# Key transposes placed behind the score products, and the first merge blocks issued as a stream of the front, in a hybrid RWKV7/FoX trunk layer

## The chip, the cores and the metric

The kernel runs on one core of one Trainium2 chip. The metric is the device time of one execution in microseconds. The kernel before was run three times: 827.68, 828.11 and 828.64 us, median 828.11 us. One further execution was profiled; its time was 826.71 us and its trace spans 824.9 us.

TensorE is called PE below, VectorE DVE, ScalarE ACT, GpSimd POOL. A PSUM "bank" is one of the accumulation buffers that PE writes and DVE or ACT reads.

## The reference, cut to what matters

```python
u = rmsnorm(h, norm_mix)
proj = u @ w_in                                  # 1024 -> RWKV features, FoX features, two gates
y_rw = rwkv7_branch(proj[..., :C_RW], ...)       # generalised delta rule, 8 heads of 64
y_fx = fox_branch(proj[..., C_RW:C_RW+C_FX], ...)# forgetting attention, 8 heads of 64
gates = sigmoid(proj[..., C_RW+C_FX:] + b_gate)
merged = gates[..., :1024] * (y_rw @ w_out_rw) + gates[..., 1024:] * (y_fx @ w_out_fx)
h = h + merged @ w_o
h = h + square(relu(rmsnorm(h, norm_mlp) @ w_up)) @ w_down
```

512 tokens and 16 meta tokens, width 1024, everything in float32. One layer.

## The kernel before, in words

Every large product is split: a weight tile `wraw` is cast on ACT to a high part `whi`, DVE subtracts to get the low part `wlo`, and PE runs three passes (`whi` with the high and the low part of the activations, `wlo` with the high part).

The first 400 us are the *front*. Forty projection jobs (function `projections`, matmuls at L582, casts at L550, subtractions at L551) form one stream. Between their matmuls stand the matmuls of the other streams: the recurrent branch with its chain over chunks, the attention, the FoX features, the group norm. Each stream is a Python generator that yields the time at which its next piece can start, by a planner's own costs; the planner takes the most urgent ready stream, and projections have the last rank but one, so that they fill gaps. This fixes PE's order by hand. The orders of DVE, ACT and the queues come from a scheduler. Nothing can overtake on PE: if the instruction at its head waits, PE stands still.

The PSUM banks have names: `pj` (two), `ch` and `py` (one each), and a ring of four called `sm` that serves everything small in the front (`psm`) and the accumulators `po` of the merge and the MLP (`ppo`). A new `sm` tile takes the bank of the fourth one before it and has to wait until that one's readers are done.

The recurrent branch works on four pairs of heads, p = 0 to 3. For a pair, `keys` makes `BK` (L922) and `KT` (L924) on DVE. `scores` goes over nine chunks in three groups of three. A group takes two `sm` banks, `sb` and `sk`, and fills them with 12 products of `BK` and `L` (L964, 24 instructions in the trace, called `psr`); DVE reads `sb` once (`Bm`, L965) and `sk` twice (`L`, L967). Then the group transposes its three chunks of `KT` on PE into a third bank (`pbt`, L971), which ACT copies out (L972, L974).

When a pair's tanh values are done (L261), `pinned` puts a load of another activation table (L268) on ACT, for the logarithms and exponentials that follow.

Behind the front stands the merge: for eight blocks m, two products of four blocks of `ys` each (the RWKV branch, br 0, and the FoX branch, br 1; 24 matmuls at L1267), a gate that comes back from DRAM (`gl`) and goes through tanh (L1262), its product on DVE (L1269), a sum on POOL (L1271) and a split (L1272, L1273). Its weights come through `load_w` (L242), which holds four half-block tiles, so two blocks; block 0 is asked for ahead of the loop, every other block in its own pass.

Of the kernel before, what the change touches and what calls it, by code (L numbers as in the profile page):

```python
# [24 lines left out]
NCH = 9  # L25
HT = T // 2
KB = 8
# [162 lines left out]
def kernel(ctx, tc, ht, x, win, par, cst, gain, lora, wout, wo, wup, wdn, out, dbg=None):  # L190
# [84 lines left out]
    def split(hi, lo, x):  # L275
        return A.copy(hi, x), V.tensor_tensor(lo, x, hi.bitcast(F32), ALU.subtract)  # L276
# [6 lines left out]
    ps = ctx.enter_context(tc.tile_pool(name="ps", bufs=2, space=PSUM))  # L283
    gates_d = [dr.tile([128, S], F32, name=f"gd{i}") for i in range(16)]
    ys = {}
    quarters = [[wdn[i][256 * c:256 * c + 256] for c in range(8)] for i in range(4)]

    with ExitStack() as st:
# [254 lines left out]
        def convert(job, raws):  # L543
# [9 lines left out]
                w.append((hi, lo))  # L553
            return job, w

        def projections(total):
            fetched, done = None, 0
            while done < total:
                if fetched is None:
                    yield lambda: 0.0 if jobs else math.inf  # L560
                    fetched = fetch(jobs.pop(0))
                cur = convert(*fetched)
                fetched = fetch(jobs.pop(0)) if jobs else None
                while cur is not None:
                    (_, _, _, begin, parts, ev, need), w = cur
                    nxt = convert(*fetched) if fetched else None
                    fetched = fetch(jobs.pop(0)) if jobs else None
                    if need is not None:
                        yield need
                    evac = begin()  # L570
                    for a0, a1 in parts:
                        po = None
                        n = 0
                        for k in range(KB):
                            if k % 2 == 0 or a1 - a0 > 300:
                                yield lambda f=po is None: max(ck.ready(*w[k // 4]), block_bank()[0] if f else 0.0)
                            if po is None:
                                tag = block_bank()[2]
                                po = ppj(tag)[:, :a1 - a0]
                                lent.extend([tag] * (tag != "pj"))  # L580
                            for a, b in passes(wk(w, k), U):
                                mm(po, a, b[:, k, a0:a1], start=n == 0, stop=n == 23)  # L582
                                n += 1
                        evac(po, slice(a0, a1))
                        if tag in lent:
                            lent.remove(tag)
                    ev.done = True
                    done += 1
                    cur = nxt

        def gate_job(i):
            def begin():
# [13 lines left out]
        def two(j, k):  # L606
            ys[4 * j + k] = t = kp.tile([128, 2, S], F32R, name="ys", tag=SLOTS[(4 * j + k) // 2], bufs=2)
            return t[:, 0, :], t[:, 1, :]

        def divided():  # L610
            yield chained[1]
            for k in range(2):
                split(*two(0, k), y_rw[:, k, :])
            for k in range(3):
                yield fox_done[k]
                split(*two(1, k), y_fx[:, k, :])
            yield normalised[1][1]
            for k in range(2, 4):
                split(*two(0, k), y_rw[:, k, :])

        forgot = Event()

# [102 lines left out]
        def attention():  # L725
# [3 lines left out]
            for p in range(4):  # L729
# [67 lines left out]
                def mixed():  # L797

                    yield lambda: max(ck.ready(vt, vm, pTm, *pT), banks(1))
                    py = psm("py")  # L800
                    for e, hs in enumerate(hss):
                        mm(py[hs], vm[32 * e:32 * e + 16, hs], pTm[32 * e:32 * e + 16, :], start=True, stop=False)
                    for j, at in enumerate((0, 4, 8, 7)):
                        for e, hs in enumerate(hss):
                            mm(py[hs, 128 * j:], vt[:, j, hs], pT[e][:, at:at + 4 - j, :].rearrange("p a b -> p (a b)"), start=False, stop=j == 3)  # L805
                        if j == 0:
                            yield lambda: 0.0
                    if p < 3:
                        A.copy(y_fx[:, p, :], py)
                    else:  # L810
                        yield chained[1]
                        split(*two(1, 3), py)

                pes = yield from scored(0)
                for i in range(4):
# [39 lines left out]
        class Pair:  # L855
# [96 lines left out]
            def scores(self):  # L952


                BK, L, KT = self.BK, self.L, self.KT
                self.bkT = bkT = kp.tile([128, NCH, 128], F32, name="bkT", bufs=2)
                self.Bm = Bm = kp.tile([128, NCH, 128], F32, name="Bm", bufs=2)
                for c0 in range(0, NCH, 3):
                    yield lambda: max(ck.ready(BK, *L) if c0 == 0 else 0.0, banks(2))
                    sb, sk = [psm("psr").rearrange("p (a b) -> p a b", b=128) for e in range(2)]  # L960
                    for j in range(3):
                        for sp, row, turn in ((sb, 0, 1), (sk, 1, -1)):
                            for (e, hs), os in zip(enumerate(hss), hss[::turn]):
                                mm(sp[os, j, :], BK[hs, c0 + j, row, :], L[e][hs, c0 + j, :], start=True, stop=True)  # L964
                    V.tensor_tensor(Bm[:, c0:c0 + 3, :], sb[:, :3, :], bc(tmask, 1, 3), ALU.mult)  # L965
                    for e, os in enumerate(hss[::-1]):
                        V.tensor_tensor(L[e][os, c0:c0 + 3, :], sk[os, :3, :], bc(tmask[os], 1, 3), ALU.mult)  # L967
                    yield lambda: max(ck.ready(KT) + 1.0, banks(1))
                    pb = psm("pbt").rearrange("p (a b) -> p a b", b=128)
                    for c in range(c0, c0 + 3):  # L970
                        nc.tensor.transpose(pb[:, c - c0, :], KT[:, c, :, :].rearrange("p a b -> p (a b)"), ident)  # L971
                    A.copy(bkT[:, c0:c0 + 3, :64], pb[:, :3, :64])  # L972
                    for hs, os in zip(hss, hss[::-1]):
                        A.copy(bkT[hs, c0:c0 + 3, 64:], pb[os, :3, 64:])  # L974

        def inverse(g, Bms, late):
# [54 lines left out]
            for n, pr_, c in cells:  # L1031
                for e, hs in enumerate(hss):
                    mm(p1[hs, n, :], Tt[qs[2 * e], c, pr_, :], W2[qs[2 * e], n, :], start=True, stop=True)
            for n, pr_, c in cells:
                for q in range(4):
                    mm(p2[qs[q], n, :], W2[qs[q], n, :], Tt[qs[q], c, pr_, half(q)], start=True, stop=True)
# [190 lines left out]
        turns.add(3, fox_features())  # L1227
        turns.add(4, divided())
        turns.add(8, projections(24 + 16))
        for i in range(16):  # L1230
            ask(9, B_GATE + i, gate_job(i), SEQ)
        with tc.manual_schedule(engines={mybir.EngineType.PE}):
# [16 lines left out]

    with ExitStack() as st:  # L1250
        mp = st.enter_context(tc.tile_pool(name="mp", bufs=1))
        ahead = [load_w(wout[0])]
        mhi = mp.tile([128, KB, S], F32R, name="mhi")
        mlo = mp.tile([128, KB, S], F32R, name="mlo")
        table["pin"] = None
        for m in range(KB):
            w = ahead.pop() if ahead else load_w(wout[m])
            pp = []
            for br in range(2):
                g = mp.tile([128, S], F32, name=f"gl{br}", bufs=2)  # L1260
                nc.sync.dma_start(g, gates_d[8 * br + m])
                act(g, g, AF.Tanh, scale=0.5)  # L1262
                po = ppo()
                n = 0
                for k in range(4 * br, 4 * br + 4):
                    for a, b in passes(wk(w, k), (0, 1)):
                        mm(po, a, ys[k][:, b, :], start=n == 0, stop=n == 11)  # L1267
                        n += 1
                V.scalar_tensor_tensor(g, g, 1.0, po, ALU.add, ALU.mult)  # L1269
                pp.append(g)  # L1270
            G.tensor_tensor(pp[0], pp[0], pp[1], ALU.add)  # L1271
            merged = act(mhi[:, m, :], pp[0], AF.Copy, scale=0.5)  # L1272
            V.scalar_tensor_tensor(mlo[:, m, :], pp[0], 0.5, mhi[:, m, :].bitcast(F32), ALU.mult, ALU.subtract)  # L1273
# [17 lines left out]

        pd = [ppo(), ppo(), ppd(), ppd()]
        for b2 in range(4):
            w = load_w(wo[0, b2])
            for i, b1 in [(i, b1) for b1 in range(2) for i in range(4)] if b2 < 3 else [(i, b1) for i in range(4) for b1 in range(2)]:
                k = 2 * b2 + b1
                for n, (a, b) in enumerate(passes(M, w[b1])):
                    mm(pd[i], a[:, k, 128 * i:128 * i + 128], b, start=k == 0 and n == 0, stop=k == 7 and n == 2)  # L1298
# [317 lines left out]
```

## Time and profile before

| | |
|---|---|
| runs | 827.68, 828.11, 828.64 us |
| profiled execution | 826.71 us; span of its trace 824.9 us |
| PE busy | 808.1 us, 98% |
| DVE busy | 607.8 us, 74% |
| ACT busy | 452.5 us, 55% |
| POOL busy | 120.0 us, 15% |
| granted PE clock | 0.99 to 1.00 in every stretch |

How to read it: PE is nearly full, so what counts is how long PE stands still and why. A row of the view of waits names the waiting engine and line, what released it, and the total, the number and the longest of such waits. A row of the timeline gives start, duration, engine, line, operation and, in brackets, the idle time ahead of it with what ended it. A row of the windows gives, for a stretch of time, its length and each engine's busy time in it.

### The profile page before, as it was taken

The page shows a single profiled execution, that of the slowest core. Times are in us where ns is not written, and L with a number is a line of the kernel's source. Part 1 is how long each engine was busy: PE and PEld are TensorE (multiplying, and loading weights), DVE is VectorE, ACT ScalarE, POOL GpSimd, SP SyncE. Part 2 cuts the span into 40 slices and gives each one's busy share as a digit, 9 for nine tenths or more (in the row PEclk, how much of TensorE's full clock was granted, in tenths as well). Part 3 has the DMA queues.
Part 4 walks back from the last instruction along what each step waited for, and adds up shares of the span by engine and source line. Part 5 has one row for each costly group of instructions (what it writes and reads, how often), then busy time and mean ns, then how long its engine had stood idle before and what let it go on. Part 6 is the DMA issues. An engine that isn't in the chain of part 4 may idle for free.

```text
span 824.9 us, 15506 instructions
## 1 busy us (share of the span) xinstructions
PE 808.1 (98%) x5886; PEld 667.3 (81%) x5886; DVE 607.8 (74%) x1196; ACT 452.5 (55%) x941; POOL 120.0 (15%) x124
## 2 busy tenths in 40 slices
PE   8999999998999999999999999999999999999998
PEld 6979887876987886778788889888888888888886
DVE  6797985687779855975267655875698678867988
ACT  7767548766575457664366534664445434543452
POOL 1021000010011000000022003100740174017400
PEclk9999999999999999999999999999999999999999
DMA  7222221211211311223687404533742365236532
GB/s 240 75 71 79 69 92 56 79 40 65 79 52 54 128 46 61 90 66 116 218 289 226 159 0 151 176 82 100 225 150 87 115 221 150 77 118 208 156 107 76
DMA packets 51483, 95.88 MB, mean 116 GB/s; under 512 B 5832, under 2 KB 7240, under 8 KB 51408
## 3 DMA queue, kind: packets, MB, share of 16 engines
q1 hardware_dynamic: 47680, 86.37, 33.0%
q0 software_dynamic: 1280, 4.20, 1.7%
q10 hardware_dynamic: 2448, 4.33, 1.5%
q8 instruction: 46, 0.75, 0.4%
q14 instruction: 29, 0.24, 0.1%
HBM read 88.56 MB, written 6.31 MB: 115 GB/s over the span
## 4 chain that ended last, share of the span: by engine, by line
PE 86%; DVE 5%; ACT 5%; issue 2%; DMA 1%; POOL 0%; DVEq 0%; ACTq 0%; SPq 0%
PE pj L582 22%; PE po L1357 21%; PE po L1484 12%; PE pd L1484 5%; PE po L1267 4%; PE po L1329 3%; PE pj L394 1%; PE pd L1298 1%; PE po L1298 1%; PE psc L751 1%; PE py L805 1%; PE psr L964 1%; PE ppt L788 1%; DVE wlo L551 1%; PE pch L1115 1%
## 5 line engine op out<-in xcount | busy, mean ns | idle before, releaser
L582 PE MATMUL pj<-uhi,whi 128*128 128x264 f32 (+1 forms) x480 | 164.3, 342 | 0.0
L582 PE MATMUL pj<-uhi,wlo 128*128 128x264 f32 (+1 forms) x480 | 153.9, 321 | 1.8 <-DVE wlo L551 1.8
L582 PE MATMUL pj<-ulo,whi 128*128 128x264 f32 (+1 forms) x480 | 153.8, 320 | 0.0
L242 DVE TENSOR_TENSOR wlo<-wraw,whi 128x512 fp32r<-128x512 f32 x84 | 81.0, 973 | 36.8 <-ACT whi L242 36.8
L582 PEld LDWEIGHTS pj<-uhi,whi 128*128 128x128 f32 x480 | 90.7, 189 | 12.9 <-issue 4.4
L582 PEld LDWEIGHTS pj<-uhi,wlo 128*128 128x128 f32 x480 | 90.7, 189 | 8.8 <-DVE wlo L551 2.2
L582 PEld LDWEIGHTS pj<-ulo,whi 128*128 128x128 f32 x480 | 91.0, 190 | 6.7 <-issue 1.6
L1357 PE MATMUL po<-zhi,whi 128*128 128x512 f32 (+1 forms) x248 | 94.8, 382 | 0.0
L1357 PE MATMUL po<-zlo,whi 128*128 128x512 f32 (+1 forms) x248 | 94.8, 382 | 0.0
L1357 PE MATMUL po<-zhi,wlo 128*128 128x512 f32 (+1 forms) x248 | 94.8, 382 | 0.0
L242 ACT CAST whi<-wraw 128x512 fp32r<-128x512 f32 x84 | 51.4, 617 | 53.5 <-PE po L1357 20.3
L551 DVE TENSOR_TENSOR wlo<-wraw,whi 128x512 fp32r<-128x512 f32 x78 | 53.8, 699 | 23.5 <-ACT whi L550 22.6
L550 ACT CAST whi<-wraw 128x512 fp32r<-128x512 f32 x78 | 47.7, 617 | 42.4 <-PE pj L582 41.7
L276 ACT CAST whi<-t 128x512 fp32r<-128x512 f32 x64 | 39.9, 624 | 44.6 <-DVE wlo L276 27.2
L1406 POOL TENSOR_TENSOR t<-traw 128x512 f32<-128x512 f32 x24 | 38.4, 1622 | 173.6 <-DMA traw<-in_wdn 173.6
L1484 PE MATMUL po<-wlo,fhi 128*128 128x512 f32 (+1 forms) x164 | 63.4, 387 | 0.2
L1484 PE MATMUL po<-whi,flo 128*128 128x512 f32 (+1 forms) x164 | 62.8, 384 | 0.0
L1484 PE MATMUL po<-whi,fhi 128*128 128x512 f32 (+1 forms) x164 | 62.3, 384 | 0.0
L276 DVE TENSOR_TENSOR wlo<-t,whi 128x512 fp32r<-128x512 f32 x64 | 43.5, 689 | 24.3 <-ACT whi L276 24.0
L1373 ACT CAST fhi<-R 128x768 fp32r<-128x768 f32 (+1 forms) x32 | 30.2, 945 | 49.1 <-DVE R L1380 26.1
L1357 PEld LDWEIGHTS po<-zlo,whi 128*128 128x128 f32 x248 | 46.6, 188 | 9.1
L1357 PEld LDWEIGHTS po<-zhi,wlo 128*128 128x128 f32 x248 | 46.6, 188 | 9.0
(330 smaller groups left out, 1706.4 us busy)
## 6 DMA issues: line engine op xcount, KB each, us to landing
wraw<-in_win SPq DMA_DIRECT2D x84, 256.0 KB, 2.6
wraw<-in_wup SPq DMA_DIRECT2D x60, 256.0 KB, 3.1
wraw<-in_wdn SPq DMA_DIRECT2D x48, 256.0 KB, 2.7
traw<-in_wdn SPq DMA_DIRECT2D x48, 256.0 KB, 3.5
gd<-gt ACTq DMA_DIRECT2D x16, 256.0 KB, 2.2
wraw<-in_wout SPq DMA_DIRECT2D x16, 256.0 KB, 3.9
gl<-gd SPq DMA_DIRECT2D x16, 256.0 KB, 3.8
traw<-in_wdn POOLq DMA_DIRECT2D x16, 256.0 KB, 3.1
```

The lines of the kernel that those rows point to most:

```text
L242: casts.append((A.copy(hi, raw), low.tensor_tensor(lo, raw, hi.bitcast(F32), ALU.subtract)))
L276: return A.copy(hi, x), V.tensor_tensor(lo, x, hi.bitcast(F32), ALU.subtract)
L550: after(A.copy(hi, raw), last["ACT"])
L551: low[0] = V.tensor_tensor(lo, raw, hi.bitcast(F32), ALU.subtract)
L582: mm(po, a, b[:, k, a0:a1], start=n == 0, stop=n == 23)
L1267: mm(po, a, ys[k][:, b, :], start=n == 0, stop=n == 11)
L1298: mm(pd[i], a[:, k, 128 * i:128 * i + 128], b, start=k == 0 and n == 0, stop=k == 7 and n == 2)
L1329: mm(po, a[:, k, 128 * i:128 * i + 128], b[:, k, :], start=n == 0, stop=n == 23)
L1357: mm(po[:, t0:t1], a, b[:, k, t0:t1], start=n == 0, stop=n == 23)
L1373: A.copy(fhi[:, j, a:b], R[:, a:b])
L1406: eng.tensor_tensor(t, sums[c, pair] if c in (T1, T2) else c, d, ALU.add)
L1484: mm(x[i][:, cols], a[:, k, left, 128 * rows:128 * rows + 128], c[:, cols], start=start and k == 0 and n == 0, stop=stop and k == n_pairs ...
```

## The change

Four edits.

1. `scores`: the transposes leave the loop over the groups. All three groups of products come first, then a loop of its own with the three transposes; the planner's due time for them loses a margin of 1 us.
2. `inverse`: between its two loops of matmuls a `yield` gives the planner a place to put other streams' work.
3. A new stream `merging`, last in rank, which starts when all forty projection jobs have been issued. It issues the matmuls of merge blocks 0 and 1 that need only the first parts of `ys`, block 0 into the two `pj` banks and block 1 into `ch` and `py`. `parted` notes which blocks of `ys` are split. The weights of block 0 are asked for ahead of the last projection job.
4. The merge loop takes over the banks begun there, works on branch 1 ahead of branch 0, and asks for weights two blocks in advance, the first blocks of `wo` among them.

```diff
 def projections(total):
+                    if done == total - 1:
+                        begun.append(load_w(wout[0]))
...
+            projected.done = True
+
+        def merging():
+            yield projected
+            for m in range(2):
+                w = begun.pop() if m == 0 else load_w(wout[m])
+                pos = []
+                for br, ks in ((0, (0, 1)), (1, (4, 5, 6, 7))):
+                    if m:
+                        yield chained[1]
+                    tag = ("pj", ("ch", "py")[br])[m]
+                    yield lambda: max(ck.ready(*w[br]), ck.ring(tag, 1, 1 if m else 2))
+                    po = ppj(tag)
+                    n = 0
+                    for k in ks:
+                        while k not in parted:
+                            yield lambda: math.inf if k not in parted else 0.0
+                        yield lambda: ck.ready(parted[k])
+                        for a, b in passes(wk(w, k), (0, 1)):
+                            mm(po, a, ys[k][:, b, :], start=n == 0, stop=n == 11)
+                            n += 1
+                    pos.append((po, n))
+                under[m] = w, pos
...
 def scores(self):
                         V.tensor_tensor(L[e][os, c0:c0 + 3, :], sk[os, :3, :], bc(tmask[os], 1, 3), ALU.mult)
-                    yield lambda: max(ck.ready(KT) + 1.0, banks(1))
+                for c0 in range(0, NCH, 3):
+                    yield lambda: max(ck.ready(KT), banks(1))
                     pb = psm("pbt").rearrange("p (a b) -> p a b", b=128)
...
 def inverse(g, Bms, late):
+            at = ck.pe
+            yield lambda: at
...
+        turns.add(8, merging())
...
         table["pin"] = None
+        line = [wout[m] for m in range(2, KB)] + [wo[0, b2] for b2 in range(4)]
+        ahead = []
         for m in range(KB):
-            w = ahead.pop() if ahead else load_w(wout[m])
+            w, pos = under.get(m) or (ahead.pop(0), [])
+            ahead.append(load_w(line.pop(0)))
             pp = []
-            for br in range(2):
+            for br in (1, 0):
...
-                po = ppo()
-                n = 0
-                for k in range(4 * br, 4 * br + 4):
+                po, n = pos[br] if pos else (ppo(), 0)
+                for k in range(4 * br + n // 3, 4 * br + 4):
...
         for b2 in range(4):
-            w = load_w(wo[0, b2])
+            w = ahead.pop(0)
+            if line:
+                ahead.append(load_w(line.pop(0)))
```

PE's instructions at the scores of pair p = 0, before (`psr` is a product of a group, `pbt` a transpose of `KT`, `pj` a projection; the bracket names the engines whose results a row waits for):

```order
L971 MATMUL pbt<-cs,KT 128x128 x3
L582 MATMUL pj<-uhi,whi 128x512
L582 MATMUL pj<-ulo,whi 128x512
L582 MATMUL pj<-uhi,wlo 128x512
L582 MATMUL pj<-uhi,whi 128x512
L582 MATMUL pj<-ulo,whi 128x512
L582 MATMUL pj<-uhi,wlo 128x512
L964 MATMUL psr<-L_662,BK 64x128
L964 MATMUL psr<-L_663,BK 64x128
L964 MATMUL psr<-L_662,BK 64x128 [waits DVE_49]
```

and in the changed kernel, from the end of the second group on, where groups one and two stand back to back:

```order
L999 MATMUL psr<-L_662,BK 64x128
L999 MATMUL psr<-L_663,BK 64x128
L587 MATMUL pj<-uhi,whi 128x512
L587 MATMUL pj<-ulo,whi 128x512
L587 MATMUL pj<-uhi,wlo 128x512
L999 MATMUL psr<-L_662,BK 64x128 [waits DVE_49]
L999 MATMUL psr<-L_663,BK 64x128
L999 MATMUL psr<-L_662,BK 64x128 [waits DVE_49,PE_49]
```

with the transposes behind the third group:

```order
L1007 MATMUL pbt<-cs,KT 128x128 [waits DVE_49]
L1007 MATMUL pbt<-cs,KT 128x128 x2
L1007 MATMUL pbt<-cs,KT 128x128 [waits DVE_49,PE_49]
L1007 MATMUL pbt<-cs,KT 128x128 x2
L587 MATMUL pj<-uhi,whi 128x512
L587 MATMUL pj<-ulo,whi 128x512
L587 MATMUL pj<-uhi,wlo 128x512
L1007 MATMUL pbt<-cs,KT 128x128 [waits DVE_49]
```

The transposes moved from between the groups to behind them, and the waits for DVE that a group carried on one row now stand on two rows of the third group and on each transpose.

DVE's instructions at pair p = 1, before (`KT` and `BK` feed the scores, `Bm` and `L` read their banks, `wlo` is a projection's low part):

```order
L921 SCALAR_TENSOR_TENSOR KT<-okk,lc 128x9x64
L306 MEMSET tm 128x1
L922 SCALAR_TENSOR_TENSOR BK<-tha,KT 128x9x64 [waits DVE_49]
L310 SCALAR_TENSOR_TENSOR ov<-pj,pr_65,tm 128x264 [waits DVE_49,Activation_49]
L924 TENSOR_TENSOR KT<-BK,P 128x1152 [waits DVE_49]
L310 SCALAR_TENSOR_TENSOR ov<-pj,pr_65,tm 128x264 [waits Activation_49]
L551 TENSOR_TENSOR wlo<-wraw,whi 128x512 [waits DMAHW5_49,PE_49]
L551 TENSOR_TENSOR wlo<-wraw,whi 128x512 [waits DMAHW6_49,PE_49]
L306 MEMSET tm 128x1 [waits DVE_49]
L965 TENSOR_TENSOR Bm<-psr,cs 128x384 [waits PE_49]
```

and now:

```order
L956 SCALAR_TENSOR_TENSOR KT<-okk,lc 128x9x64
L552 TENSOR_TENSOR wlo<-wraw,whi 128x512 [waits DMAHW3_49,PE_49,Activation_49]
L957 SCALAR_TENSOR_TENSOR BK<-tha,KT 128x9x64 [waits DVE_49]
L307 MEMSET tm 128x1
L552 TENSOR_TENSOR wlo<-wraw,whi 128x512 [waits DMAHW5_49,PE_49,Activation_49]
L959 TENSOR_TENSOR KT<-BK,P 128x1152 [waits DVE_49]
L311 SCALAR_TENSOR_TENSOR ov<-pj,pr_65,tm 128x264 [waits DVE_49]
L311 SCALAR_TENSOR_TENSOR ov<-pj,pr_65,tm 128x264 [waits Activation_49]
L552 TENSOR_TENSOR wlo<-wraw,whi 128x512 [waits DMAHW6_49,PE_49]
L307 MEMSET tm 128x1 [waits DVE_49]
L1000 TENSOR_TENSOR Bm<-psr,cs 128x384 [waits PE_49]
```

One subtraction more stands ahead of `BK`, and one between `BK` and the second `KT`.

ACT's instructions behind the scores of pair p = 2, before (`sg` and `tha` are the tanh values of the next pair, `pup` their bank):

```order
L261 ACT_TABLE_LOAD [waits PE_49]
L261 ACTIVATE sg<-pup,prh 128x264 [waits Pool_49]
L261 ACTIVATE tha<-pup,prh 128x264 [waits PE_49]
L550 CAST whi<-wraw 128x512 [waits DMAHW4_49,PE_49]
L261 ACTIVATE sg<-pup,prh 128x264 [waits PE_49]
L261 ACTIVATE tha<-pup,prh 128x264 [waits PE_49]
L793 COPY pTm<-ppm 48x128 [waits PE_49]
```

and now:

```order
L261 ACT_TABLE_LOAD [waits PE_49]
L261 ACTIVATE sg<-pup,prh 128x264 [waits Pool_49]
L261 ACTIVATE tha<-pup,prh 128x264 [waits PE_49]
L268 ACT_TABLE_LOAD
L261 ACT_TABLE_LOAD
L261 ACTIVATE sg<-pup,prh 128x264 [waits PE_49]
L261 ACTIVATE tha<-pup,prh 128x264 [waits PE_49]
L720 ACT_TABLE_LOAD
L720 ACTIVATE fsq<-pssq,eps 128x512 [waits Activation_49]
```

The logarithm of the FoX features (`fsq<-pssq`), which stood elsewhere before, now falls here, and table loads stand between and behind the tanh halves. In all, ACT holds 11 table loads before and 15 now.

ACT at the start of the merge, before (`whi` are the casts of merge weights):

```order
L242 CAST whi<-wraw 128x512 [waits DMAHW1_49,DVE_49,PE_49]
L242 CAST whi<-wraw 128x512 [waits DMAHW3_49,DVE_49,PE_49]
L1262 ACT_TABLE_LOAD [waits DMAHW6_49,DMAHW1_49]
L1262 ACTIVATE gl_5402<-gl_5402 128x512 [waits Pool_49]
L1262 ACTIVATE gl_5419<-gl_5419 128x512 [waits DMAHW2_49]
```

and now:

```order
L242 CAST whi<-wraw 128x512 [waits DMAHW1_49,DVE_49,PE_49]
L1303 ACT_TABLE_LOAD [waits DMAHW6_49,DMAHW1_49]
L1303 ACTIVATE gl_5467<-gl_5467 128x512 [waits Pool_49]
L242 CAST whi<-wraw 128x512 [waits DMAHW3_49,DVE_49,PE_49]
L1303 ACTIVATE gl_5471<-gl_5471 128x512 [waits DMAHW2_49]
```

The second cast of a block moved behind the table load and the first tanh. On PE the matmuls of block 0 still follow the last projection directly in both kernels.

More of the change, by code (lines that the diff above doesn't have):

```diff
@@ L285 @@
     ys = {}
+    under = {}
     quarters = [[wdn[i][256 * c:256 * c + 256] for c in range(8)] for i in range(4)]
@@ L554, in convert @@
             return job, w
+        begun, parted, projected = [], {}, Event()
         def projections(total):
@@ L589, in projections @@
                     cur = nxt
+            projected.done = True
[20 more added lines that the diff above has]
+                under[m] = w, pos
+            return
         def gate_job(i):
@@ L608, in two, with part @@
             return t[:, 0, :], t[:, 1, :]
+        def part(j, k, y):
+            hi, lo = two(j, k)
+            split(hi, lo, y)
+            parted[4 * j + k] = lo
         def divided():
@@ L612, in divided @@
             for k in range(2):
-                split(*two(0, k), y_rw[:, k, :])
+                part(0, k, y_rw[:, k, :])
             for k in range(3):
                 yield fox_done[k]
-                split(*two(1, k), y_fx[:, k, :])
+                part(1, k, y_fx[:, k, :])
             yield normalised[1][1]
             for k in range(2, 4):
-                split(*two(0, k), y_rw[:, k, :])
+                part(0, k, y_rw[:, k, :])
         forgot = Event()
@@ L811, in mixed @@
                         yield chained[1]
-                        split(*two(1, 3), py)
+                        part(1, 3, py)
                 pes = yield from scored(0)
@@ L1251 @@
         mp = st.enter_context(tc.tile_pool(name="mp", bufs=1))
-        ahead = [load_w(wout[0])]
         mhi = mp.tile([128, KB, S], F32R, name="mhi")
```

## The prediction

> **What bounds the kernel now.** I read the page first, then the view of PE's waits, the table of windows, and the timeline at the places that the change touches.
>
> ```profile
> PE 808.1 (98%) x5886; PEld 667.3 (81%) x5886; DVE 607.8 (74%) x1196; ACT 452.5 (55%) x941; POOL 120.0 (15%) x124
> PE 86%; DVE 5%; ACT 5%; issue 2%; DMA 1%; POOL 0%; DVEq 0%; ACTq 0%; SPq 0%
> ```
>
> PE is busy 808.1 of 824.9 us, and the number of its matmuls does not change. So the time moves only by what PE waits. These are its waits:
>
> ```profile
> PE pbt L971 <- DVE KT L924: 2.1, 2, 1.3
> PE pj L582 <- DVE wlo L551: 1.8, 1, 1.8
> PE pch L1115 <- DVE Rs L1111: 1.7, 3, 1.2
> PE po L1267 <- DVE gl L1269: 1.0, 1, 1.0
> PE psr L964 <- DVE Bm L965: 0.4, 1, 0.4
> PE psr L964 <- DVE BK L922: 0.3, 1, 0.3
> ```
>
> The columns are total, number and longest in us. The change is aimed at the first (transposes that wait for `KT`) and the fourth (a merge accumulator that waits for a bank). Together they hold 3.1 us, which is all that it can remove there. The windows show where these waits lie: length, then PE busy, and DVE busy behind PEld.
>
> ```profile
> 48.00:60.00 12.00, 10.20 (x110) 7.48 (x110) 10.88 (x19) 5.53 (x14) 2.42 (x3) 1.00 0.35 110
> 84.00:95.00 11.00, 9.49 (x119) 7.67 (x118) 10.79 (x19) 6.08 (x17) 1.53 (x4) 1.00 0.24 75
> 210.00:232.00 22.00, 22.00 (x234) 20.62 (x233) 17.06 (x42) 13.43 (x33) 0.48 (x1) 1.00 0.19 61
> 250.00:262.00 12.00, 10.61 (x125) 8.55 (x124) 11.32 (x18) 6.41 (x18) 1.25 (x2) 1.00 0.12 45
> ```
>
> They hold the scores of p = 0, 1, 2 and 3. PE stands 1.8 us in the first (the `wlo` wait, ahead of the scores, whose order does not change), 1.51 in the second, nothing in the third, 1.39 in the fourth. In the first, second and fourth DVE is busy 10.8 to 11.3 of 11 to 12 us: at the scores DVE has no slack, and what PE asks of it a microsecond sooner it gets late.
>
> **The change part by part.**
>
> *Scores.* Four banks serve as a ring. Before, the order was group 1 (banks 0, 1), transpose (2), group 2 (3, 0), transpose (1), group 3 (2, 3), transpose (0): a group found one bank long free and needed at most `Bm` of the group before it. Now the order is groups 1 (0, 1), 2 (2, 3), 3 (0, 1), then transposes (2, 3, 0). Group 3 must wait for `Bm` of group 1 on its first product and for both `L` of group 1 on its third; the first transpose for `Bm` and the second for both `L` of group 2. Those are the rows with DVE waits in the order above. The prices, at p = 1:
>
> ```profile
> 84.03 0.76 DVE L922 SCALAR_TENSOR_TENSOR BK<-tha,KT 128x576 f32<-128x576 f32 x1
> 84.84 0.89 PE L964 MATMUL psr<-L,BK 64*64 64x128 f32 x24 [0.28 <-DVE BK L922]
> 85.10 1.35 DVE L924 TENSOR_TENSOR KT<-BK,P 128x1152 f32<-128x1152 f32 x1
> 86.51 0.55 PE L971 MATMUL pbt<-cs,KT 128*128 128x128 f32 x3 [0.78 <-DVE KT L924]
> 86.77 1.28 DVE L551 TENSOR_TENSOR wlo<-wraw,whi 128x512 fp32r<-128x512 f32 x2
> 87.98 0.55 DVE L965 TENSOR_TENSOR Bm<-psr,cs 128x384 f32<-128x384 f32 x1
> 88.56 1.12 DVE L967 TENSOR_TENSOR L<-psr,cs 64x384 f32<-64x384 f32 x2
> 88.59 0.87 PE L964 MATMUL psr<-L,BK 64*64 64x128 f32 x20 [0.45 <-DVE Bm L965]
> ```
>
> A group takes 0.89 us on PE, `Bm` 0.55 and the two `L` 1.12 on DVE: DVE needs 1.7 us for what PE makes in 0.9. Before, 18 projections between the groups filled the difference, now 12 do and none stands between groups 1 and 2.
>
> p = 1. `KT` ends at 84.0 and one `wlo` (0.64, half of the pair above) now stands ahead of `BK`, so `BK` ends near 85.4. PE comes 0.6 us sooner than before (5 projections fewer ahead) and waits 1.1. Groups 1 and 2 end at 87.1, six projections at 87.95. DVE meanwhile has `wlo`, `KT`, two `ov` and a `wlo`, and starts the first `Bm` near 88.95, done 89.5: group 3 waits 1.5. Both `L` are done at 90.6: 1.0 more. The second transpose waits 0.6 for `L` of group 2. Sum 4.2 us against 1.5 before: **+2.7**. The wait for `KT` itself is gone. Low end +0.5, if the scheduler's `wlo` rows fall outside the gap; high end +3.5.
>
> p = 0:
>
> ```profile
> 54.85 0.40 PE L582 MATMUL pj<-ulo,whi 128*128 128x512 f32 x1
> 55.08 0.40 PE L582 MATMUL pj<-uhi,wlo 128*128 128x512 f32 x1
> 55.41 0.89 PE L964 MATMUL psr<-L,BK 64*64 64x128 f32 x24
> ...
> 54.02 0.55 DVE L965 TENSOR_TENSOR Bm<-psr,cs 128x384 f32<-128x384 f32 x1
> 54.60 1.12 DVE L967 TENSOR_TENSOR L<-psr,cs 64x384 f32<-64x384 f32 x2
> ```
>
> Nothing waited before. A 512-wide projection takes a step of 0.23 us, and where the array's form changes (to `psr`) the step is 0.33, so a change costs 0.1. Now group 3 comes three projections after group 2, 2.5 us after the scores began at 52.5; both `L` of group 1 end at 55.6. PE waits about 0.6 there, 0.6 at the second transpose and 0.2 at the third, less two changes of array form of 0.1: **+1.1**, bounds 0 and +2.
>
> p = 2. Groups 2 and 3 and two transposes stand together with no projection between. PE runs through them in about 2.2 us, DVE needs 1.7 for each group: the second transpose waits about 1.0 for both `L`, less one change of form: **+0.9**, bounds 0 and +1.7.
>
> p = 3:
>
> ```profile
> 234.10 1.07 PE L802 MATMUL py<-pTm,vm 16*64 16x512 f32 x4
> 235.11 2.37 PE L805 MATMUL py<-pT,vt 128*64 128x512 f32 x16
> ...
> 253.46 0.52 PE L971 MATMUL pbt<-cs,KT 128*128 128x128 f32 x3 [1.31 <-DVE KT L924]
> ```
>
> Between `keys`' products and the scores PE now has attention products like these (3.4 us) and six projections more (0.7), and `pssq` (about 1) has left, so that the scores start some 3 us later against DVE, and the wait of 1.31 for `KT` goes; about 0.5 for the second transpose stays: **-0.9**, bounds -1.4 and +1.1 (the upper end has PE arrive as early as before).
>
> *ACT behind the scores of p = 2.*
>
> ```profile
> 225.55 1.28 ACT L261 ACT_TABLE_LOAD   x1
> 226.85 0.48 ACT L261 ACTIVATE sg<-pup,prh 128x264 f32<-128x264 f32 x1
> 227.23 0.47 ACT L261 ACTIVATE tha<-pup,prh 128x264 f32<-128x264 f32 x1
> 229.04 0.28 PE L582 MATMUL pj<-uhi,wlo 128*128 128x264 f32 x1
> 229.16 0.29 PE L582 MATMUL pj<-uhi,whi 128*128 128x264 f32 x1
> ```
>
> A table load takes 1.28 us. Four more are 5.1 us of ACT, which has room on the whole but not here. The FoX square sum `pssq` now takes its ring bank between the two tanh halves, its logarithm stands behind three more loads, and the product `pg` takes that same bank four tiles later. ACT, from the last transpose: first tanh bank ready 2.4, load 1.3, two tanh 0.9, two loads 2.6, two tanh 0.9, load 1.3, logarithm 0.6: about 10.2 us with hand-overs. PE, from the same point: 42 narrow projections at 0.12 (steps of these rows),  tanh products, `pssq`, transposes: about 8.4 at `pg`. PE waits **+1.9**; bounds 0 (if the group norm's products slip later) and +2.5 (the next projection's bank, read by DVE after ACT, is then about 0.4 late too).
>
> [...]
>
> *The yield in* `inverse` has no instruction of its own. It lets the planner put work between its two loops. Of the waits of the chain (1.7 us) the longest, 1.2, then has six projections instead of three ahead of it, and DVE's copy stands earlier: **-1.0**, bounds -1.7 and +1, since it shifts every later piece of the recurrent stream too.
>
> *Merge.* PE order shows that no front work lies beside the begun blocks: they follow the last projection as block 0 did. So "inside the front" itself brings nothing. What changes is the bank and the casts.
>
> ```profile
> 402.75 0.62 ACT L242 CAST whi<-wraw 128x512 fp32r<-128x512 f32 x1 [1.51 <-PE po L1267]
> 405.48 0.62 ACT L242 CAST whi<-wraw 128x512 fp32r<-128x512 f32 x1 [2.10 <-PE po L1267]
> 409.43 1.28 ACT L1262 ACT_TABLE_LOAD   x1 [3.33 <-DMA gl<-gd]
> 410.73 1.15 ACT L1262 ACTIVATE gl<-gl 128x512 f32<-128x512 f32 x2
> 411.39 1.28 DVE L1269 SCALAR_TENSOR_TENSOR gl<-gl,po 128x512 f32<-128x512 f32 x2 [4.57 <-ACT gl L1262]
> 412.13 0.73 PE L1267 MATMUL po<-ys,whi 128*128 128x512 f32 x2 [1.03 <-DVE gl L1269]
> ```
>
> Before, the fifth accumulator waits 1.03 us for the first gate, whose tanh waits for a DRAM round trip and a table load. Two blocks now sit in other banks, so that this wait is gone. But the weight casts of block 2, both ahead of the load before, are now split around it, and the half that PE wants first (branch 1) is the one behind. A merge matmul takes 0.23 us. The first cast needs the tile that the rest of block 0 frees 9.5 us into the merge; then cast 0.6, load 1.3, tanh 0.6, cast 0.6: 12.6 to 12.9. PE reaches block 2 after 48 matmuls, at 10.9. It waits 2.0, and 0.2 for `wlo`, which DVE makes behind a gate product: +2.2 less 1.0, **+1.2**. Bounds -1.0 (gate and cast both in time) and +1.9. Later blocks have 2 us of slack, and weights asked for two blocks ahead wait for the same four tiles.
>
> **Sum:** +2.7 +1.1 +0.9 -0.9 +1.9 -1.0 +1.2 = +5.9 us. The profiled execution took 826.71 (span 824.9 and 1.8 around it), which would become 832.6; it lies 1.4 under the median of the runs, 828.11, so for the median I say **834.0**.
>
> **The rivals.**
>
> *It does as meant* (ends on the other side). DVE reads the banks in time: if `Bm` and `L` of group 1 start 1.7 us sooner against PE than I have it, group 3 and the second transpose find their banks free, and the two table-bound waits are covered by projections. Then only the 2.1 of `KT` and the 1.0 of `po` go: 825.0. For it speaks that p = 2 had no wait before; against it the windows, where DVE is 91 to 98% busy at p = 0, 1 and 3. It decides where DVE's backlog at `BK` is under one `wlo` (0.64).
>
> *Even.* The same banks wait, but half as long, and the chain gives back its 1.7: about 828.
>
> *Scores only.* The scores cost their +3.8 as reckoned, but the waits at `pg` and at block 2 are covered (0 and -1.0): 828.1 +3.8 -1.0 -1.0 = 829.9, or 831 without the chain's gain.
>
> *A convoy on ACT.* The loads behind p = 2 also push the casts `whi` and the copies after them. A cast queued behind `pg`'s stall stops the next projection job, which costs up to the three loads left, 3.8 us: 838.
>
> **How the numbers follow.** The forecast has 0.50 (its own range 831.5 to 836.5), as meant 0.14, even 0.11, scores only 0.14, the convoy 0.11. About 0.2% (1.7 us) is what this kernel's runs can tell from no change. Faster than 826.4: "as meant" and a sliver of "even", 0.15. Within 0.2%: 0.10. Slower: 0.75. The range 826.0 to 838.0 leaves out most of "as meant" and half of the convoy.
>
> **What would show it.** In the changed kernel's waits: a wait of `psr` (L999) for `Bm` or `L` (L1000, L1002) near 55, 88 to 90 us; `pbt` (L1007) for `L`, none for `KT`; 15 table loads; `pg` (L1209) released by ACT near 230 us; `po` (L1307) released by ACT's cast (L242) or DVE's `wlo` about 11 us into the merge, none for `gl`. The forecast is wrong if DVE reaches the first `Bm` before PE reaches group 3 at p = 1, or if the logarithm at L720 ends before PE comes to `pg`.

## The result and the profile after

The changed kernel takes 848.15 us (847.5 to 851.7, 4 runs) against 827.89 us before: 1.0255 times as long, 95% interval 1.0224 to 1.0285. Forecast was 834.0 with a range to 838. The direction was right, the size was not: the loss is 20 us and not 6. Executions far longer than the others of the same kernel (1132 to 2653 us) are left out of every time and ratio below.

First the page of the changed kernel's profile (span and busy time of each engine), then PE's longest waits but for those of the first 16 us:

```profile
span 849.9 us, 15512 instructions
PE 819.8 (96%) x5886; PEld 673.1 (79%) x5886; DVE 604.5 (71%) x1196; ACT 458.6 (54%) x945; POOL 121.8 (14%) x124
```

```profile
PE pyt L1206 <- DVE ysq L1201: 8.3, 1, 8.3
PE pj L587 <- DVE wlo L552: 2.5, 2, 1.8
PE pbt L1007 <- DVE Bm L1000: 2.0, 2, 1.4
...
PE psr L999 <- DVE Bm L1000: 1.3, 1, 1.3
PE pch L1147 <- DVE uv L1177: 1.2, 1, 1.2
PE psr L999 <- DVE L L1002: 1.2, 2, 0.8
PE psc L786 <- ACT yT L1214: 0.9, 1, 0.9
PE po L1307 <- ACT whi L242: 0.9, 2, 0.7
PE po L1307 <- DVE wlo L242: 0.8, 1, 0.8
PE psc L786 <- DVE tm L307: 0.8, 1, 0.8
...
PE pch L1153 <- DVE Rs L1149: 0.5, 1, 0.5
PE pbt L1007 <- DVE L L1002: 0.5, 2, 0.3
```

Two things stand out. The wait for `KT` and the wait of `po` for the gate are gone, as the change meant. But the first row is one wait of 8.3 us, the longest of the kernel, at an instruction that the diff does not touch: `pyt`, the group norm's transposes of its first half. And PE's busy time grew by 11.7 us (808.1 to 819.8) with the same 5886 instructions. Idle time (span less busy) grew by 13.3 us, from 16.8 to 30.1. The two make the 25.0 us by which the profiled span grew (this profiled execution, 851.7 us, is the longest of the four; the median lies 3.5 lower).

Part of the growth of the busy time is the clock. The trace's clock records give PE half clock in four stretches of the changed kernel (from 92, 184, 225 and 249 us); half of PE's busy time in them, 7.5 us, is lost work. (In the second stretch a 512-wide projection followed the one before it by 0.42 to 0.43 us, L587 from 193.63 us on, and by 0.23 from 194.48 us on, at full clock.) The kernel before has one such stretch, 3.4 us from 203 us on, with 1.7 us lost. (So the clock of 0.99 to 1.00 "in every stretch", given ahead of the prediction, is not exact: from 180 to 240 us it was 0.97.) The clock thus holds 5.8 of the 11.7 us; what the other 5.9 us of busy time come from was not taken apart.

The timeline at the wait, PE and then DVE, of the changed kernel (start, duration, engine, line, operation, idle time ahead and its releaser):

```profile
178.58 0.40 PE L1132 MATMUL py<-y_fx,Bm 64*64 64x64 f32 x8
189.68 1.08 PE L1206 MATMUL pyt<-cs,ysq 128*128 128x128 f32 x4 [8.35 <-DVE ysq L1201]
...
175.33 0.68 DVE L1191 TENSOR_REDUCE st<-y_rw 128x8 f32<-128x512 f32 x1
180.10 0.68 DVE L1197 TENSOR_REDUCE st<-ysq 128x8 f32<-128x512 f32 x1
182.03 0.75 DVE L957 SCALAR_TENSOR_TENSOR BK<-tha,KT 128x576 f32<-128x576 f32 x1
183.24 1.35 DVE L959 TENSOR_TENSOR KT<-BK,P 128x1152 f32<-128x1152 f32 x1
186.84 0.68 DVE L552 TENSOR_TENSOR wlo<-wraw,whi 128x512 fp32r<-128x512 f32 x1
188.84 0.69 DVE L1201 TENSOR_TENSOR ysq<-y_rw,rsgy 128x512 f32<-128x512 f32 x1
```

The group norm's work on DVE, from its first reduction (175.3) to `ysq` (done 189.5), stretches over 14 us, because the next pair's `BK`, `KT` and low parts stand between its steps. The same two rows of the kernel before:

```profile
173.10 0.68 DVE L1153 TENSOR_REDUCE st<-y_rw 128x8 f32<-128x512 f32 x1
186.82 0.69 DVE L1163 TENSOR_TENSOR ysq<-y_rw,rsgy 128x512 f32<-128x512 f32 x1
197.77 0.65 PE L1168 MATMUL pyt<-cs,ysq 128*128 128x128 f32 x4
```

DVE's part is as long as before (14.2 us now, 14.4 before). What moved is PE's: before, `pyt` came 10.3 us after `ysq` was done; now it is the head of PE's queue 8.3 us before, and nothing behind it ran in that time (PE busy 0.00 from 184 to 188 us, below).

The windows around it (length, PE busy, PEld, DVE, ACT, POOL; third column from the end: the granted clock):

```profile
184.00:188.00 4.00, 0.00 (x0) 0.00 (x0) 3.94 (x11) 0.00 (x0) 1.89 (x2) 0.53 0.22 66
188.00:192.00 4.00, 2.32 (x12) 2.12 (x12) 1.79 (x7) 0.73 (x2) 0.00 (x0) 0.50 0.21 66
192.00:196.00 4.00, 4.00 (x28) 3.06 (x27) 1.97 (x6) 1.90 (x6) 0.00 (x0) 0.69 0.03 6
196.00:200.00 4.00, 4.00 (x37) 1.83 (x37) 1.24 (x3) 0.64 (x2) 0.00 (x0) 1.00 0.09 28
```

While PE waited here, its granted clock fell to one half, and it stayed there for about 5 us after the work went on: by the clock records from 184.2 to 194.5 us. PE was busy for 4.8 us of that, so 2.4 us of work are lost at this place.

### The profile page after: what moved, and what is told of

Its sections match the earlier page's. It is cut to its first block, busy times and chain, and to the rows that moved or that the text cites. A ratio compares the mean times of both kernels' runs of the same rounds, so it can differ in the third digit from the quotient of the medians.

```text
span 849.9 us, 15512 instructions
## 1 busy us (share of the span) xinstructions
PE 819.8 (96%) x5886; PEld 673.1 (79%) x5886; DVE 604.5 (71%) x1196; ACT 458.6 (54%) x945; POOL 121.8 (14%) x124
## 4 chain that ended last, share of the span: by engine, by line
PE 62%; ACT 4%; DVE 3%; DMA 3%; issue 1%; POOL 0%; SPq 0%; DVEq 0%; ACTq 0%; POOLq 0%
PE po L1399 21%; PE pj L587 12%; PE po L1526 12%; PE pd L1526 5%; PE po L1371 3%; DMA gl<-gd 2%; PE pd L1340 1%; PE po L1340 1%; PE py L840 1%; PE psc L786 1%; DMA gd<-gt 1%; PE po L1307 1%; PE ppt L823 1%; PE pd L1361 0%; DVE L L1002 0%
## 5 line engine op out<-in xcount | busy, mean ns | idle before, releaser
L587 PE MATMUL pj<-uhi,whi 128*128 128x264 f32 (+1 forms) x480 | 166.2, 346 | 0.0
L587 PE MATMUL pj<-uhi,wlo 128*128 128x264 f32 (+1 forms) x480 | 155.1, 323 | 2.5 <-DVE wlo L552 2.5
L587 PE MATMUL pj<-ulo,whi 128*128 128x264 f32 (+1 forms) x480 | 155.0, 323 | 0.0
L242 DVE TENSOR_TENSOR wlo<-wraw,whi 128x512 fp32r<-128x512 f32 x84 | 76.9, 924 | 41.5 <-ACT whi L242 41.5
L587 PEld LDWEIGHTS pj<-uhi,whi 128*128 128x128 f32 x480 | 92.0, 192 | 13.1 <-issue 4.8
L587 PEld LDWEIGHTS pj<-uhi,wlo 128*128 128x128 f32 x480 | 91.8, 191 | 9.9 <-DVE wlo L552 3.2
L587 PEld LDWEIGHTS pj<-ulo,whi 128*128 128x128 f32 x480 | 92.0, 192 | 6.5 <-issue 1.6
L552 DVE TENSOR_TENSOR wlo<-wraw,whi 128x512 fp32r<-128x512 f32 x78 | 54.9, 712 | 29.1 <-ACT whi L551 28.6
L1399 PEld LDWEIGHTS po<-zhi,whi 128*128 128x128 f32 x248 | 46.6, 188 | 9.0
```

Of the source, the lines that this page charges most:

```text
L242: casts.append((A.copy(hi, raw), low.tensor_tensor(lo, raw, hi.bitcast(F32), ALU.subtract)))
L552: low[0] = V.tensor_tensor(lo, raw, hi.bitcast(F32), ALU.subtract)
L1399: mm(po[:, t0:t1], a, b[:, k, t0:t1], start=n == 0, stop=n == 23)
```

## The experiments

Each kernel ran beside the kernel before on the same chip. Two theories to begin with: A, the place of the transposes sends the planner into an order in which `pyt` comes too early, and the idle PE then loses clock; B, the merge edits carry the loss.

**The scores edit alone** (in the kernel before; no yield, no merge edits):

```diff
-                    yield lambda: max(ck.ready(KT) + 1.0, banks(1))
+                for c0 in range(0, NCH, 3):
+                    yield lambda: max(ck.ready(KT), banks(1))
```

> The kernel before with the first edit alone (transposes of KT in a loop of their own behind the three groups, without the 1 us margin); no yield in inverse, no merging stream, merge loop as before. Theory A (this edit makes the planner place the group norm's transposes pyt some 8 us ahead of what DVE can deliver, and the idle PE is then given a lower clock): 842 to 850 us, a pyt wait of 7 to 9 us near 185 us, 15 ACT table loads, granted clock under 0.993. Theory B (the merge edit carries the loss): 829 to 832 us, no pyt wait.

Measured: 848.02 us, ratio 1.0244 (1.0217 to 1.0271): all of the loss. Of PE's waits in this run, by line:

```profile
PE pyt L1169 <- DVE ysq L1164: 8.3, 1, 8.3
...
PE pbt L972 <- DVE Bm L965: 2.0, 2, 1.4
...
PE psr L964 <- DVE Bm L965: 1.3, 1, 1.3
```

So neither the yield in `inverse` nor the merge has a part in it that can be told from none (848.0 without them, 848.2 with them).

**The merge edits alone:** scores and `inverse` as before, the rest as changed.

> The kernel before with the merge edits alone (stream merging, branch 1 first, weights two blocks ahead); scores and inverse as before. Theory A: 827 to 830 us (the 1.0 us wait for the gate goes, waits of up to 1.7 us for casts and low parts at block 2 come). Theory B: 840 to 850 us.

Measured: 828.96 us, ratio 1.0017 (1.0004 to 1.0029). Theory B falls. The gate wait of 1.0 went and this came:

```profile
PE po L1304 <- ACT whi L242: 1.2, 2, 0.8
```

**`pyt` later.** In the changed kernel, for the first group norm only:

```diff
-            yield lambda: max(ck.ready(ysq), banks(2))
+            yield lambda: max(ck.ready(ysq) + (4.0 if (g, c0) == (0, 0) else 0.0), banks(2))
```

> The changed kernel, but the planner is told that the first group norm's ysq is ready 4 us later, so that pyt stands later in PE's order. Theory A: the 8.3 us wait goes and with it 2 to 6 us of lowered clock: 834 to 839 us. Theory B, or if the wait only moves to the next instruction that needs the same DVE work: 845 to 850 us.

Measured: 828.21 us, ratio 1.0006 (0.9997 to 1.0015), mean granted clock 0.999. I had expected 834 to 839. One number in the planner gives the whole 20 us back, more than the wait and the clock at that place, since the plan behind it is another one too (11 table loads and not 15, and no wait of `pbt` for `Bm` over 0.3). Here `pyt` finds its data:

```profile
190.02 0.69 DVE L1201 TENSOR_TENSOR ysq<-y_rw,rsgy 128x512 f32<-128x512 f32 x1
196.73 0.60 PE L1206 MATMUL pyt<-cs,ysq 128*128 128x128 f32 x4
```

Its waits at the scores are still there (`psr` for `Bm` and `L`):

```profile
PE psr L999 <- DVE L L1002: 2.0, 3, 0.8
...
PE psr L999 <- DVE Bm L1000: 1.3, 1, 1.3
```

It is also the only variant whose merge began beside front work (its first product stands at 395.8 us, with attention and group norm products behind it). It shows no `po` wait at all, but neither do the runs with branch 0 first, below, so that this alone need not be the reason.

**Filling the wait.** The changed kernel with work for PE ahead of `pyt`, which the planner does not see; its result is overwritten by the transposes:

```diff
+            if (g, c0) == (0, 0):
+                ck.read()
+                for i in range(36):
+                    nc.tensor.matmul(pt.rearrange("p a b -> p (a b)"), lhsT=uhi[:, 0, 0:128], rhs=uhi[:, 0, 0:512], start=True, stop=True)
+                ck.seen = len(nc.cur_bb.bb.instructions)
```

> The changed kernel with 36 extra products of 0.23 us (8.2 us of PE work whose result is overwritten) directly ahead of the first pyt, hidden from the planner; every other instruction stands where it stood. If the wait costs more than its own length because PE's clock is lowered around it: 843 to 846.5 us, no clock under 0.95 between 184 and 200 us. If the idle time has no such effect: 848 us, as the changed kernel. If the filling comes on top of the wait: 856 us.

Measured: 843.14 us, ratio 1.0186 (1.0169 to 1.0203), where the changed kernel has 1.0255. The filler took the place of the wait, and the clock stayed up:

```profile
179.55 8.36 PE L1208 MATMUL pyt<-uhi 128*128 128x512 f32 x36
188.08 0.63 PE L1211 MATMUL pyt<-cs,ysq 128*128 128x128 f32 x4 [0.18 <-DVE ysq L1201]
...
184.00:188.00 4.00, 3.90 (x18) 2.89 (x16) 3.70 (x12) 0.00 (x0) 1.43 (x2) 1.00 0.37 129
188.00:192.00 4.00, 3.92 (x35) 3.32 (x35) 1.39 (x4) 2.09 (x7) 0.00 (x0) 1.00 0.03 9
192.00:196.00 4.00, 4.00 (x36) 1.65 (x35) 1.71 (x4) 1.22 (x3) 0.00 (x0) 1.00 0.07 5
```

8.4 us more work in the same place makes the kernel 5.0 us faster by the medians, 5.7 by the ratios (3 to 9, estimated from their two intervals). So about a quarter of the loss goes with the clock and not with the time itself that PE spends at `pyt`: the executions of the changed kernel have a mean granted clock of 0.988 to 0.990, those of the filled one 0.998 to 0.999.

Not all of it lies at `pyt`. Set side by side instruction by instruction, the two profiled executions end 9.0 us apart. Of this, 2.1 us arise at `pyt`. Another 3.2 arise at 225 and 249 us, where the changed kernel has a dip of the clock and the filled one has none behind the same waits, and 1.6 in the first 20 us, ahead of the filler; the rest arises at 300 us and in the merge. Why the two later dips stayed away is not shown.

**The margin alone.** The kernel before without `+ 1.0` on the transposes' due time, the transposes where they were:

> The kernel before with one thing changed: the 1 us margin on the transposes' due time is gone, the transposes stay between the groups. If the place of the transposes makes the loss (theory A): 826 to 829 us, no pyt wait. If the missing margin makes it: 840 us or more.

Measured: 826.59 us, ratio 0.9992 (0.998 to 1.0004): no difference. But for four instructions in the first 60, PE's order is that of the kernel before, so between the groups the margin decides nothing. The loss needs the new place. Whether it would also come there with the margin kept was not run.

**The planner's cost model.** The changed kernel with

```diff
-            eng = "Pool" if out.startswith("wlo") else str(x.engine).split(".")[-1]
+            eng = str(x.engine).split(".")[-1]
```

> The changed kernel, but the planner's cost model books the low parts wlo on DVE, where they run, and no longer on POOL; the kernel's own work is the same. Theory A1 (the plan puts pyt too early because the planner thinks DVE free of the low parts): no pyt wait over 2 us, 826 to 834 us. Theory A2 (it is too early for another reason, the planner's insertion of group norm work into gaps of DVE that the real order does not have): a pyt wait of over 4 us, 838 to 850 us.

Measured: 853.49 us, ratio 1.0317 (1.0299 to 1.0335). Neither expectation held. The first `pyt` now finds its data, which were done 2.9 us before, and a later one waits 1.5 us, as A1 says. But the time rose, because two other instructions took its part:

```profile
PE pw L1063 <- DVE AX L1049: 12.6, 2, 7.4
PE ppm L821 <- ACT pm L806: 2.1, 1, 2.1
...
PE pyt L1206 <- DVE ysq L1201: 1.5, 1, 1.5
```

A model that books more truly moved the long wait from the group norm to `inverse`. So the booking of the low parts is not the cause by itself; the planner's DVE and the real one differ in other ways, which were not taken apart.

**The first pair as before.** The changed kernel, but for p = 0 the transposes stay between the groups:

```diff
+                    if self.p < 1:
+                        yield from turned(c0, 1.0)
+                if self.p >= 1:
+                    for c0 in range(0, NCH, 3):
+                        yield from turned(c0, 0.0)
```

(`turned` holds the transposes and their copies.)

> The changed kernel, but for the first pair of heads (p = 0) the transposes stay between the groups with their margin; pairs 1 to 3, the yield and the merge edits are as changed. If one shift of a few microseconds at 55 us sends the planner into the bad order 125 us later: 827 to 831 us, no pyt wait, 11 table loads. If the loss belongs to all four pairs' places: 840 to 848 us.

Measured: 832.12 us, ratio 1.0057 (1.0037 to 1.0077), 1 us above the range expected; no `pyt` wait, 11 table loads. The place of one pair's transposes, at 55 us, decides about a wait at 181 us. What is left above the kernel before is not idle time: PE stands still for 16.7 us in all, before 16.8. There are new waits at the scores and at two other places, but others have gone. PE's busy time is 813.9 us and not 808.1. Three dips of the clock, with 5.1 us of work lost against 1.7, hold 3.4 of these 5.8 us; the rest was not taken apart. The new waits:

```profile
PE psr L1008 <- DVE L L1011: 2.1, 3, 0.8
PE pssq L718 <- ACT fsq L694: 1.9, 1, 1.9
...
PE psr L1008 <- DVE Bm L1009: 1.3, 1, 1.3
PE po L1313 <- DVE wlo L242: 1.2, 2, 0.8
```

**Two candidates.** Transposes behind the scores for pairs 2 and 3 only, with branch 0 ahead of branch 1 in the merge:

> A candidate: transposes behind the scores for pairs 2 and 3 alone, all else as changed, but branch 0 ahead of branch 1 in the merge, so that the cast ahead of the table load is the one that PE wants first. From the merge-only run (829.0) the 1.2 us of cast waits and the 1.3 us KT wait of pair 3 go: 826 to 827.5 us, no po wait over 0.3. If new waits take their place: 828 to 830 us.

Measured: 830.82 us, ratio 1.0043 (1.0029 to 1.0058): the `po` wait went, as expected, but the time missed. All its waits together are no longer than before; its PE is busy 813.9 us and not 808.1, with a granted clock of 0.993.

The changed kernel with the third group's banks due 2 us later in the plan, and branch 0 first:

```diff
-                    yield lambda: max(ck.ready(BK, *L) if c0 == 0 else 0.0, banks(2))
+                    yield lambda: max(ck.ready(BK, *L) if c0 == 0 else 0.0, banks(2) + (2.0 if c0 == 6 else 0.0))
```

> The changed kernel, but the planner is told that the banks for the third score group come free 2 us later, so that 9 wide or 18 narrow projections stand between groups 2 and 3 where 3 or 6 stood; and branch 0 ahead of branch 1 in the merge. If the bank waits at the scores are what I took them for (DVE's Bm and L of group 1), the psr waits at 57 and 90 us, 3 us together, go or fall under 0.5, the KT and po waits stay away and pyt stands behind its data: 824 to 827 us. If the order breaks somewhere else instead: 828 to 835 us.

Measured: 831.2 us, ratio 1.0047 (1.0032 to 1.0062). At the scores the wait for `Bm` is gone and 0.7 for `L` is left, so these waits were what they were taken for; `KT`, `po` and `pyt` do not wait. But a new one came (`psr` for `BK`, 1.4; the 1.5 us at `psc` stand in the kernel before too), and two dips of the clock (0.62 from 52 to 56 us; 0.65 and 0.50 from 204 to 212 us). All waits together are no longer than before (15.9 us idle against 16.8), and PE's busy time is 813.6 us and not 808.1. Faster than before it is not.

**The merge with branch 0 first** (the merge-only kernel with `for br in (0, 1)`):

> The merge-only kernel (829.0) with one thing put back: branch 0 ahead of branch 1. If the 1.2 us po wait for a cast came from the order of the branches: no po wait over 0.3 and 826.5 to 828 us. If it came from asking for weights two blocks ahead: a po wait of 1 us stays and 829 us.

Measured: 827.73 us, ratio 1.0006 (0.9995 to 1.0016), and no `po` wait. The cast wait came from the order of the branches. With it mended the merge edits cost nothing, and they bring nothing that can be measured either.

No variant beat the kernel before.

## Why the prediction was wrong, point by point

*What bounds the kernel:* right in kind. PE's waits count, and 13.3 of the 25.0 us are waits. But "the time moves only by what PE waits" left out PE's busy time, which itself grew by 11.7 us, 5.8 of them by the clock. This step gave idle time no price beyond its own length, and there it failed: filling the wait won back about 5 us. The list of waits that stands under "These are its waits" also leaves out, beside two at the start, 1.5 us at `psc` (L751) and 0.6 at `py` (L1143); in the changed kernel `psc` waits 1.7 us, in two pieces.

*The part that failed most is the list of places.* I priced the places of the diff, of the table loads and of the merge, and took the rest of the front as it was: the sum has no term for it, and no reason is given for that. The order is planned anew from the first changed yield on, and `pyt` moved from 10 us behind its data to 8.3 us ahead of it. No rival held that either. The rows that show it were there to be read: `pyt`'s row, that it now carries a wait for DVE which it did not carry before, and the 14 us that DVE takes from the first reduction to `ysq` in the trace of before.

*Scores.* The waits came at the pairs where they were put, and most on the banks that were named. p = 0: forecast +1.1, measured 0.6. p = 1: waits of 2.8 instead of 4.2, so +1.3 and not +2.7; 0.7 of the 2.8 is a `wlo` ahead of the scores, and the waits for `BK` and at the second transpose did not come. p = 2: 2.0 instead of 1.0, and for `Bm` instead of `L`. p = 3: the wait of 1.3 for `KT` went and 0.3 for `L` came, -1.0 against -0.9. Together +2.9 against +3.8. Lines of the changed kernel at p = 0, 1 and 2:

```profile
57.26 0.87 PE L999 MATMUL psr<-L,BK 64*64 64x128 f32 x20 [0.37 <-DVE L L1002]
58.88 0.52 PE L1007 MATMUL pbt<-cs,KT 128*128 128x128 f32 x3 [0.27 <-DVE L L1002]
...
90.88 0.43 PE L999 MATMUL psr<-L,BK 64*64 64x128 f32 x4 [1.27 <-DVE Bm L1000]
92.13 1.55 PE L999 MATMUL psr<-L,BK 64*64 64x128 f32 x20 [0.81 <-DVE L L1002]
...
223.91 0.55 PE L1007 MATMUL pbt<-cs,KT 128*128 128x128 f32 x3 [1.38 <-DVE Bm L1000]
225.09 0.85 PE L1007 MATMUL pbt<-cs,KT 128*128 128x128 f32 x3 [0.63 <-DVE Bm L1000]
```

The row at 92.13 shows the other price: 20 score products in 1.55 us, after 2 us of waiting, where the first row has 0.87 for the same 20. By the clock records PE had half clock from 92.06 to 95.48 us.

*ACT behind p = 2,* +1.9: wrong. The four loads came, at 1.28 us each, but `pg` did not wait. It began while the logarithm was still to come, so the bank that I gave it was not the one it took:

```profile
236.15 0.37 PE L1209 MATMUL pg<-lhi,lw 128*128 128x256 f32 x1
236.00 1.28 ACT L720 ACT_TABLE_LOAD   x1
237.30 0.69 ACT L720 ACTIVATE fsq<-pssq,eps 128x512 f32<-128x512 f32 x1
```

Around the load at L720 there was no other delay: the activation ahead of it ended 0.02 us before its start, and the logarithm started 0.02 us after its end.

*The yield,* -1.0: nothing that can be seen. The scores edit without it takes the same time; the chain's waits changed from `Rs` (1.7) to `uv` (1.2) and `Rs` (0.5), and did so in the run without the yield too. The yield alone was not run.

*Merge,* +1.2: right in kind, +0.7 in size. The wait for the gate went (1.0), waits for the cast and the low part came (0.9 and 0.8). At block 2, 11 us into the merge, PE waited 0.7 for the cast and not 2.0. The other 1.0 came some 40 us into it, at blocks to which the prediction gave 2 us of slack. Alone, the merge edits cost 0.17% (1.4 us), and putting branch 0 first takes the wait away.

So of the 25.0 us between the two profiled executions the priced places hold 3.6 (the scores' 2.9 and the merge's 0.7). The wait of `pyt` holds 8.3, other waits 1.4, the clock 5.8 (2.4 of it behind `pyt`), and 5.9 us of PE's busy time stay open. The failed step is the missing term: 8.3 us at `pyt` and the clock lost behind it, where the sum has nothing.

## What to carry to other kernels

Where a planner sets the order, a diff has no edge: compare the two orders over the whole stage, and look first for rows that now wait for an engine and did not before, then read from the old trace when their data are ready. A plan made with costs that differ from the real engine's can lose its slack far from an edit: here the transposes' place at 55 us moved `pyt`, at 181 us, from 10.3 us behind its data to 8.3 us ahead of them, and 4 us more in one due time put it back. Why the planner's own times moved `pyt` so far was not found.

## What the runs showed of the hardware

After the long wait at `pyt` PE was slow for a while. After 8.3 us of waiting the granted clock was 0.50 to 0.69 in the next windows, up to 194.5 us, and with the same 8.3 us filled by products whose result nobody uses it was 1.00. Dips followed shorter waits too, but not each time: after 1.27 and 0.81 us of waiting at p = 1, and after 1.38 and 0.63 at p = 2, the clock dipped in the changed kernel,

```profile
224.00:228.00 4.00, 3.37 (x17) 3.13 (x18) 2.57 (x5) 1.96 (x7) 0.00 (x0) 0.65 0.21 66
228.00:232.00 4.00, 4.00 (x26) 2.98 (x25) 1.15 (x3) 3.49 (x7) 0.00 (x0) 0.93 0.12 42
```

which is 1.7 us of work lost (4 times 0.35 and 4 times 0.07), as much as 3.4 us at half clock. The clock records agree: 3.41 us at half clock. In all these traces, but for the records that run past a trace's end, a dip lasted that long or two or three times as long (6.83 from 300 us on with the scores edit alone, 10.24 from 184 us on in the changed kernel). In the run with the filled wait, the same 2.0 us of `pbt` waits at p = 2 brought no dip (granted clock 1.00 from 216 to 232 us). In the run with the scores edit alone, the dip at 300 us (0.53 from 300 to 304 us, 0.62 from 304 to 308) followed 4 us in which PE stood still for only 0.24. So for the short waits it is not shown that the wait is the cause, nor why the same waits bring a dip in one run and none in another.
